# Seven quarter products in six of the 22 half-pairs of an FFN's second matmul

## The chip, the cores and the metric

The kernel runs on one NeuronCore of one Trainium2 chip. The metric is the device time of one execution in microseconds; the time of a kernel is the median of its runs. In code and profile PE is TensorE, PEld its weight loads, DVE VectorE, ACT ScalarE, POOL GpSimd, SP SyncE (which issues the DMAs).

## The reference

One decoder layer on 512 tokens of width 1024, in fp32: a half-step SwiGLU FFN, a token mixer (HGRN2 and mLSTM heads), and a second half-step FFN, each between a pre-norm and a post-norm. What the change touches is the second product of both FFNs, `@ w_out`:

```python
def swiglu_ffn(x, w_in, w_out):          # D_MODEL 1024, D_FF 2816
    gate, up = jnp.split(x @ w_in, 2, axis=-1)
    return (jax.nn.silu(gate) * up) @ w_out

x = x + 0.5 * rms_norm(swiglu_ffn(rms_norm(x, norm_pre[l, 0]), ffn1_w_in[l], ffn1_w_out[l]), norm_post[l, 0])
mixed = token_mixer(rms_norm(x, norm_pre[l, 1]), ...)
x = x + rms_norm(mixed, norm_post[l, 1])
x = x + 0.5 * rms_norm(swiglu_ffn(rms_norm(x, norm_pre[l, 2]), ffn2_w_in[l], ffn2_w_out[l]), norm_post[l, 2])
```

## The kernel before

**Products in two parts.** Each fp32 operand is split into a high part (its cast to fp32r) and a low part (the rest). A product of two such operands is three matmuls: high by high, high by low, low by high (`mm3`, lines 125 to 129). The cast is made by ACT and the residual by DVE: for a weight tile in `split` (L209 the cast, L211 the residual), for a tile of the hidden activations h in `h_tile` (L672 and L673).

**The stages.** `ffn_in` makes gate and up for 11 pairs of 128-row slices of the hidden width (PAIRS = 11), by a scheme of seven products of 256-wide quarters (`prod`, matmuls at L489; `after`, with DVE's additions at L508); GpSimd adds weight quarters for it (L223). The result h lies in `hf`, 22 slices of 128 x 512 tokens. `ffn_out` multiplies it by w_out.

**ffn_out before.** The output's 1024 columns are done in two halves. A half has four PSUM banks (`acc`), one for each tile of 128 tokens. It adds up over the 11 pairs of slices: one pair in one half is a half-pair, so an FFN has 22 of them. A half-pair needs one w tile (two slices by 512 columns, 512 KB) and one h tile, and is 24 matmuls of 128 x 512: four token tiles, two slices, three matmuls each (L127, L128, L129). After the first pair of half 0 the last group of `ffn_in` (`prod("p4", 10)`, 24 matmuls) is done. After half 0, `post0` takes the squares (ACT, L354) and the product with the gain (DVE, L383) from the four banks. The last four pairs of half 1 are done token tile by token tile, with the post-norm and the work of the next stage in between (`last`).

**Buffers.** Loads of w_out go to a ring of five raw tiles (`raw2`), issued by SP. Split weights go to four slots (WBUF = 4): `pull` splits ahead until four are ready or in use, `drop` frees one. Split h tiles go to a ring of three (tag `s`); `more(n)` makes them ahead. `xq` is four tiles that hold the split input of `ffn_in`, free in `ffn_out`. PSUM has eight banks; `ps()` gives the next in turn.

**Order.** Outside the kernel's first part, which is ordered by hand, the order of each engine's instructions is set by a scheduler when the program is built. Each engine then takes its own queue in that order, and waits on semaphores for the other engines.

Of the kernel before, what the change touches and what calls it, by code (L numbers as in the profile page):

```python
# [8 lines left out]
F32 = mybir.dt.float32  # L9
F32R = mybir.dt.float32r  # L10
AF = mybir.ActivationFunctionType
ALU = mybir.AluOpType
PSUM = bass.MemoryType.PSUM

P = 128
T = 512
D = 1024
FF = 2816
NT = T // P
ND = D // P  # L20
NF = FF // P
EPS = 1e-6
RAW, WBUF, PAD, LATE, NEAR = 3, 4, 128, 112, 48
PAIRS = NF // 2
HALF = T // 2
# [4 lines left out]
HQ, HF, HI, HG, MQ, MV, MO, MG = 0, 512, 1024, 1536, 2048, 2560, 3072, 3584  # L30
LEVELS = (1, 64, 32, 16, 8, 4, 2)
TINY = 1e-37
I32 = mybir.dt.int32


# [15 lines left out]
class Load:  # L51


    def __init__(self, key, src, a, b, ring="raw", depth=3, ahead=3, group=None):
        self.key, self.src, self.a, self.b, self.ring, self.depth, self.ahead = key, src, a, b, ring, depth, ahead
        self.group = group


class Item:

    def __init__(self, key, loads, rows=None, adds=(), dst=None):
        self.key, self.loads, self.rows, self.adds, self.dst = key, loads, rows, adds, dst
        self.reads = {key, *(k for pair in adds for k in pair)}


class Layer:
# [26 lines left out]
    def col(self, n=1):  # L95
        return self.sp.tile([P, n], F32, tag=f"col{n}", bufs={1: 12}.get(n, 4), name=self.name("col"))
# [89 lines left out]
    def split(self):  # L186

        nc = self.nc
        it = self.items.popleft()
        raw = self.raw[it.key]  # L190
        _, a, b = raw.shape
        if it.dst:
            w = it.dst()
        else:
            if self.wt is None:
                self.wt = self.wp.tile([P, 2 * D * WBUF + PAD], F32R, name="w")

            taken = {(n, late) for n, late, _ in self.slot.values()}
            fit = [(n, late) for late in (True, False) for n in self.free if (n - 1 if late else n + 1, not late) not in taken]
            n, late = next(f for f in fit if not f[1] or (it.key[0] == "mix" and b == 512))  # L200
            self.free.remove(n)
            o = PAD + 2 * D * n - 16 * late
            w = self.wt[:, o : o + 2 * D].rearrange("p (b k t) -> p b k t", b=2, k=a)
            self.slot[id(w)] = n, late, w
        hi, lo = self.both(w)
        self.ready.append((w, it.dst is not None))
        rows = it.rows
        if rows is None:
            nc.scalar.copy(hi, raw)  # L209
            yield  # L210
            nc.vector.tensor_tensor(lo, raw, hi.bitcast(F32), op=ALU.subtract)  # L211
        else:
            for j in range(a):
                nc.scalar.activation(hi[:, j], raw[:, j], AF.Copy, scale=rows[:, j : j + 1])
            yield
            for j in range(a):
                nc.vector.scalar_tensor_tensor(
                    lo[:, j], raw[:, j], rows[:, j : j + 1], hi[:, j].bitcast(F32), op0=ALU.mult, op1=ALU.subtract
                )
        with self.behind(*self.hold):  # L220
            for out, other in it.adds:
                o, c = self.raw[out], self.raw[other]
                nc.gpsimd.tensor_tensor(o, o, c, op=ALU.add)  # L223
        self.load_due(self.done)
        self.done += 1
        yield
# [44 lines left out]
    def two(self, dst, i, src):  # L271

        v = slice((i % 2) * P, (i % 2 + 1) * P)
        self.nc.scalar.copy(dst[:, 0, :, v], src)
        self.nc.vector.tensor_tensor(dst[:, 1, :, v], src, dst[:, 0, :, v].bitcast(F32), op=ALU.subtract)  # L275
# [398 lines left out]
        return t  # L674

    def ffn_out(self, gpost_row, scale, after, trans, head):
        NK2, LAST = PAIRS, 4
        seq = [k2 for _ in range(2) for k2 in range(NK2)]
        hs = self.hs
        made = [len(hs)]  # L680

        def more(n):
            while made[0] < min(n, len(seq)):
                k2 = seq[made[0]]
                last = made[0] == len(seq) - 1
                dst = self.xq[3].rearrange("p b k t -> p b (k t)").rearrange("p b (k t) -> p b k t", k=2) if last else None
                hs.append(self.h_tile(k2, dst))
                made[0] += 1

        def out_mm(ps, w, h, k2, i):  # L690
            for kk in range(2):
                k = 2 * k2 + kk
                s = slice(i * P, (i + 1) * P)
                self.mm3(ps, h[:, 0, kk, s], h[:, 1, kk, s], w[:, 0, kk, :], w[:, 1, kk, :], k == 0, k == NF - 1)

        g = self.gain("gpost", gpost_row)
        ys = []
        n = 0
        for half in range(2):
            acc = [self.ps() for _ in range(NT)]  # L700
            for k2 in range(NK2 - LAST if half else NK2):
                more(n + 2)
                w = self.pull()
                more(n + 3)
                h = hs.popleft()
                for i in range(NT):
                    out_mm(acc[i], w, h, k2, i)
                self.drop(w)
                n += 1
                if n == 1:  # L710
                    self.prod("p4", PAIRS - 1)
                    self.after("p4", PAIRS - 1)
                self.lag()
            if half == 0:
                ys = [self.post0(acc[i], g, scale) for i in range(NT)]
        ws = []
        for k2 in range(NK2 - LAST, NK2):
            ws.append((k2, self.pull()))
            more(n + 1)
            n += 1  # L720

        def mm(i):
            for m, (k2, w) in enumerate(ws):
                out_mm(acc[i], w, hs[m], k2, i)
                if i == NT - 1:
                    self.drop(w)
                yield LAST - 1 - m

        self.last(mm, ys, acc, g, after, trans, head)


# [73 lines left out]
    def ffn_items(self, name, w_in, w_out):  # L805

        made = []
        place = {"p1": "a", "p2": "c", "p3": "d", "p4": "a", "p5": "a", "p6": "a", "p7": "b"}
        place.update({"c1": "a", "c2": "c", "c3": "b", "c4": "d"})
        adds = {}  # L810
        for t in range(1, PAIRS):
            if t >= HEAD:
                v1, v3 = ("p1", t), ("p4", t - 1)
            elif t > 1:
                v1, v3 = ("p3", t - 1), ("p6", t - 1)
            else:
                v1, v3 = ("p1", 1), ("p1", 2)
            for at, o, i in ((("p5", t), "a", "d"), (("p6", t), "a", "c"), (v1, "a", "b"), (v3, "b", "d")):
                adds.setdefault(at, []).append(((name, t, o), (name, t, i)))

        def load(t, r, group=None):
            ring = ("raw", 3) if t % 2 == 0 and r != "c" else ("raw2", 5)
            k, c = int(r in "cd"), int(r in "bd")
            c0 = c * FF + t * 2 * P
            src = w_in[k * 4 * P : (k + 1) * 4 * P, c0 : c0 + 2 * P].rearrange("(k p) f -> p k f", p=P)
            return Load((name, t, r), src, KH, 2 * P, *ring, 8, group)

        own = {("p1", t): [load(t, r) for r in "abdc"] for t in range(2, PAIRS)}
        own["c1", 0] = [load(t, r, None if (t, r) == (0, "d") else name) for t in range(2) for r in "acbd"]

        stay = {"c1": 1, "c3": 2, "c4": 0}
        for p, t in ORDER:
            if p[0] == "e":
                continue
            dst = (lambda n=stay[p]: self.stay[n]) if p in stay else None
            made.append(Item((name, t, place[p]), own.get((p, t), ()), None, adds.get((p, t), ()), dst))
        for h in range(2):
            for k2 in range(PAIRS):
                src = w_out[k2 * 2 * P : (k2 + 1) * 2 * P, h * 512 : (h + 1) * 512].rearrange("(k p) d -> p k d", p=P)
                key = (name, "out", h, k2)  # L840
                made.append(Item(key, [Load(key, src, 2, 512, "raw2", 5, 8)]))
                if h == k2 == 0:
                    made.append(Item((name, PAIRS - 1, "a"), ()))
        return made

    def small_params(self):

# [31 lines left out]
        self.tiny = mc.tile([P, 1], F32, name="tiny")  # L879
        nc.gpsimd.memset(self.tiny, TINY)  # L880
        self.one = mc.tile([P, 1], F32, name="one")
        nc.gpsimd.memset(self.one, 1.0)

    def masks(self, mc, mb):
# [7 lines left out]
        n16 = len(LEVELS)  # L892
        self.mask = mb.tile([P, n16, 16], I32, name="mask")
        self.eye = mb.tile([P, 32], I32, name="eye")
        wide = self.st("wide", dt=I32)[:, : 64 * n16].rearrange("p (n c) -> p n c", n=n16)
# [663 lines left out]
```

## Time and profile before

| | |
|---|---|
| median of 3 runs | 937.52 us (937.2 to 938.1) |
| the profiled execution | 936.74 us, its span 935.0 us |
| mean granted TensorE clock | 0.998 |
| TensorE busy | 926.7 us (99%) |
| VectorE, ScalarE, GpSimd busy | 700.1, 468.7, 289.9 us |
| w_out loads | 44 of 512 KB, 3.9 us to landing (median) |
| first FFN's ffn_out | 225.3 to about 350 us of the span |

Rows of the timeline are: start, duration, engine, line, operation, output and input with their shapes, and in brackets how long the engine stood idle before it and what ended that. Rows of groups are: line, engine, operation, names, shapes, count, then busy us, mean ns of one, idle us before them and what ended it. Rows of the chain that ended last are: start, length, engine, line, count. Ends of matmuls are modelled, so the distance between starts is the pace. Rows of windows give the stretch, its length, the busy time and count of PE, PEld, DVE, ACT and POOL, the granted clock, the DMA share and GB/s.

### The profile page before, as it was taken

The numbers are of one execution on the slowest core, as the hardware profiler recorded it, in microseconds if no ns is written. First come the engines' busy times: TensorE is split into PE (matmuls) and PEld (weight loads), VectorE is DVE, ScalarE is ACT, GpSimd is POOL, SyncE is SP. The second block draws the span as 40 slices with busy tenths as digits, with TensorE's granted clock in tenths as the row PEclk, the third lists the DMA queues.
The fourth block names the chain that finished last, engine by engine and source line by source line (L and its number), as shares of the span: only waits on it lengthen the run. The fifth ranks groups of instructions, "written<-read, shape, count | busy, mean of one in ns | idle before, by whom it ended". The sixth has DMA issues, their size and how long they took to land.

```text
span 935.0 us, 16820 instructions
## 1 busy us (share of the span) xinstructions
PE 926.7 (99%) x7021; PEld 850.6 (91%) x7021; DVE 700.1 (75%) x785; ACT 468.7 (50%) x639; POOL 289.9 (31%) x225
## 2 busy tenths in 40 slices
PE   9999999999999999999999999999999999999997
PEld 7999999999888889998888888999999999988885
DVE  6798999998545466688766655887999999844543
ACT  7645445455334345987654254853444454534431
POOL 3535555661000027000020301445455655100001
PEclk9999999999999999999999999999999999999999
DMA  9243334425323005422423135213333422332202
GB/s 318 89 136 114 113 97 131 128 99 158 113 91 106 7 3 126 108 83 70 136 70 113 46 108 185 90 46 113 114 111 117 134 91 91 116 110 91 91 0 91
DMA packets 81992, 97.10 MB, mean 104 GB/s; under 512 B 4178, under 2 KB 61558, under 8 KB 81915
## 3 DMA queue, kind: packets, MB, share of 16 engines
q1 hardware_dynamic: 81306, 94.44, 32.4%
q8 instruction: 55, 0.90, 0.4%
q0 software_dynamic: 320, 1.06, 0.3%
q10 hardware_dynamic: 288, 0.52, 0.2%
q14 instruction: 23, 0.18, 0.1%
HBM read 93.90 MB, written 2.11 MB: 103 GB/s over the span
## 4 chain that ended last, share of the span: by engine, by line
PE 97%; DVE 1%; POOL 1%; issue 1%; ACT 1%; DVEq 0%; POOLq 0%; ACTq 0%
PE ps L489 46%; PE ps L127 13%; PE ps L129 13%; PE ps L128 13%; PE ps L434 6%; PE ps L268 1%; PE ps L1058 1%; POOL col L355 0%; PE ps L1328 0%; PE ps L1131 0%; PE ps L1296 0%; PE ps L116 0%; ACT junk L354 0%; PE ps L123 0%; PE ps L1097 0%
## 5 line engine op out<-in xcount | busy, mean ns | idle before, releaser
L211 DVE TENSOR_TENSOR w<-raw,w 128x1024 fp32r<-128x1024 f32 x214 | 364.2, 1710 | 129.5 <-ACT w L209 129.5
L209 ACT CAST w<-raw 128x1024 fp32r<-128x1024 f32 x214 | 223.9, 1052 | 305.6 <-PE ps L129 104.5
L223 POOL TENSOR_TENSOR raw<-raw,raw 128x1024 f32<-128x1024 f32 x80 | 221.0, 2763 | 171.8 <-DVE w L211 161.3
L489 PE MATMUL ps<-xq,w 128*128 128x256 f32 x2016 | 238.1, 277 | 0.0
L489 PEld LDWEIGHTS ps<-xq,w 128*128 128x128 f32 x2016 | 233.7, 188 | 0.2
L489 PE MATMUL ps<-sq,w 128*128 128x256 f32 x1440 | 171.0, 277 | 0.0
L489 PEld LDWEIGHTS ps<-sq,w 128*128 128x128 f32 x1440 | 167.4, 188 | 0.0
L129 PE MATMUL ps<-w,hs 128*128 128x512 f32 x336 | 131.0, 390 | 0.0
L127 PE MATMUL ps<-w,hs 128*128 128x512 f32 x336 | 130.9, 390 | 0.0
L128 PE MATMUL ps<-w,hs 128*128 128x512 f32 x336 | 130.8, 389 | 0.0
L127 PE MATMUL ps<-w,xq 128*128 128x512 f32 x208 | 83.2, 400 | 0.1
L128 PE MATMUL ps<-w,xq 128*128 128x512 f32 x208 | 81.0, 390 | 0.0
L129 PE MATMUL ps<-w,xq 128*128 128x512 f32 x208 | 81.0, 391 | 0.0
L129 PEld LDWEIGHTS ps<-w,hs 128*128 128x128 f32 x336 | 63.1, 188 | 13.8 <-DVE hs L673 0.7
L127 PEld LDWEIGHTS ps<-w,hs 128*128 128x128 f32 x336 | 63.1, 188 | 13.0
L128 PEld LDWEIGHTS ps<-w,hs 128*128 128x128 f32 x336 | 63.1, 188 | 12.8
L355 POOL TENSOR_SCALAR col<-col 128x1 f32<-128x1 f32 x24 | 10.5, 437 | 198.8 <-ACT junk L354 198.6
L434 PE MATMUL ps<-xq,w 128*128 128x256 f32 x480 | 55.8, 278 | 0.0
L434 PEld LDWEIGHTS ps<-xq,w 128*128 128x128 f32 x480 | 55.4, 188 | 0.2 <-issue 0.2
L673 DVE TENSOR_TENSOR hs<-hf,hs 128x1024 fp32r<-128x1024 f32 x42 | 51.1, 1217 | 0.0
L355 POOL TENSOR_SCALAR col<-col,col 128x1 f32<-128x1 f32 x24 | 10.0, 418 | 119.5 <-ACT junk L354 119.2
L129 PEld LDWEIGHTS ps<-w,xq 128*128 128x128 f32 x208 | 39.0, 188 | 8.8 <-DVE xq L275 0.3
(233 smaller groups left out, 939.5 us busy)
## 6 DMA issues: line engine op xcount, KB each, us to landing
raw<-in_ffn_w_in_dram SPq DMA_DIRECT2D x88, 512.0 KB, 4.4
raw<-in_ffn_w_out_dram SPq DMA_DIRECT2D x44, 512.0 KB, 3.9
raw<-in_w_mix_in_dram SPq DMA_DIRECT2D x28, 512.0 KB, 3.8
raw<-in_w_mix_out_dram SPq DMA_DIRECT2D x8, 512.0 KB, 3.7
out_dram<-xs SPq DMA_DIRECT2D x8, 256.0 KB, 2.1
xs<-in_x_dram SPq DMA_DIRECT2D x6, 256.0 KB, 6.2
gpost<-in_norm_post_dram SPq DMA_DIRECT2D x3, 512.0 KB
gpre<-in_norm_pre_dram SPq DMA_DIRECT2D x2, 512.0 KB, 4.1
```

Of the source, the lines that this page charges most:

```text
L127: mm(ps, sh, mh, start=start, stop=False, **kw)
L128: mm(ps, sh, ml, start=False, stop=False, **kw)
L129: mm(ps, sl, mh, start=False, stop=stop, **kw)
L209: nc.scalar.copy(hi, raw)
L211: nc.vector.tensor_tensor(lo, raw, hi.bitcast(F32), op=ALU.subtract)
L223: nc.gpsimd.tensor_tensor(o, o, c, op=ALU.add)
L268: self.nc.tensor.transpose(pt[:, c * P : (c + 1) * P], src[:, k * P : (k + 1) * P], self.ident)
L355: nc.gpsimd.tensor_scalar(m, ss, s2 / D, b, op0=ALU.mult, op1=ALU.add)
L434: mm(ps[:, u0:u1], w[:, a, k, :], self.xop(k, b, u0, u1), start=k + n + m == 0, stop=k == ND - 1 and n == 2, skip_group_check=True,)
L489: self.nc.tensor.matmul(ps[:, c], wb[b][:, k, v], left[d][:, k, :], start=first and a + n + k == 0, stop=n == 2 and k == KH - 1, skip_grou ...
L673: self.nc.vector.tensor_tensor(t[:, 1], src, t[:, 0].bitcast(F32), op=ALU.subtract)
L1058: nc.tensor.matmul(sc[r, o : o + u.stop - u.start], k8[:, m, r], q8[:, m, u], start=True, stop=True, skip_group_check=True)
```

## The change

A table OUT now names for both halves the order and kind of the half-pairs: `p` as before, `k` and `s` by seven quarter products. Half 0 has k3 and k4, half 1 has k3, s1, k4 and s2: six per FFN, twelve in the kernel. Such a half-pair is a 2 x 2 block product (tokens in two halves, the pair's two slices, columns in two halves) made of seven products of blocks, with 42 matmuls 256 wide (`seven`). It needs a second weight tile `wt` of sums of the weight's quarters (`w_sums`: after the first split of a raw tile, four subtractions by DVE in that raw tile, which is then split again into a second slot) and a second h tile of sums (`s_tile`: four DVE steps in `hf`, then a cast and a residual). For k pairs both h tiles are kept in `xq` for both halves.

Products 2, 3 and 4 add straight into the output's banks. Products 1, 5, 6 and 7 add up, over all fast pairs of a half, in four more banks (`sums`). After the last fast pair of a half `gather` makes four terms of them (one ACT copy, four DVE additions, into slices of `hf` that are no longer needed), and at the second p pair after that, p6 in both halves, DVE adds the terms to the output's banks, one addition per bank ahead of that bank's matmuls. `holes()` after half 0 turns the bank ring by four.

No load is added and GpSimd gets no work. The pairs p7 to p10 of half 1 are done as before.

```diff
+OUT = ("p0 p1 p2 k3 k4 p5 p6 p7 p8 p9 p10".split(), "p0 k3 s1 k4 s2 p5 p6 p7 p8 p9 p10".split())
...
 (split)
+        if it.then:
+            it.then(raw)
         self.load_due(self.done)
...
 (ffn_out, more)
+                if kind == "k":
+                    if h == 0:
+                        kept[k2] = self.h_tile(k2, homes.popleft()), self.s_tile(k2, homes.popleft())
+                    hs.append(kept[k2])
+                elif kind == "s":
+                    hs.append((self.h_tile(k2), self.s_tile(k2)))
...
+        def seven(acc, sums, w, wt, h, hs_, stop):
+            tok = lambda q, t: slice(HALF * q + P * t, HALF * q + P * (t + 1))
+            col = lambda q: slice(HALF * q, HALF * (q + 1))
+            for p, a, ka, qa, b, kb, qb in (
+                (1, h, 0, 0, w, 0, 0), (5, hs_, 1, 1, wt, 0, 0), (6, hs_, 0, 0, wt, 1, 1), (7, hs_, 0, 1, wt, 0, 1),
+                (2, h, 1, 0, w, 1, 0), (3, hs_, 1, 0, w, 1, 1), (4, h, 1, 1, wt, 1, 0),
+            ):
+                fresh = p not in sums
+                if fresh and p in (1, 5, 6, 7):
+                    sums[p] = self.ps()
+                for t in range(2):
+                    if p in sums:
+                        out = sums[p][:, col(t)]
+                    else:
+                        out = acc[2 * (p == 4) + t][:, col(p == 3)]
+                    for m, (x, y) in enumerate(((0, 0), (0, 1), (1, 0))):
+                        self.nc.tensor.matmul(
+                            out, a[:, x, ka, tok(qa, t)], b[:, y, kb, col(qb)],
+                            start=p in sums and fresh and t + m == 0, stop=stop and m == 2, skip_group_check=True,
+                        )
+
+        def gather(sums, pairs):
+            x, y = (self.hf[:, 2 * k : 2 * k + 2, :].rearrange("p t (c v) -> p t c v", c=2) for k in pairs)
+            u = self.sp.tile([P, D], F32, tag="xn", bufs=1, name=self.name("u2"))[:, :512]
+            two = lambda t: t.rearrange("p (t v) -> p t v", t=2)
+            self.nc.scalar.copy(x[:, :, 0], two(sums[1]))
+            add(two(u), two(sums[6]), x[:, :, 0])
+            add(x[:, :, 1], two(sums[5]), two(u))
+            add(y[:, :, 0], two(sums[7]), two(u))
+            add(y[:, :, 1], two(sums[5]), y[:, :, 0])
+            return [t[:, i].rearrange("p c v -> p (c v)") for t in (x, y) for i in range(2)]
...
         for half in range(2):
             acc = [self.ps() for _ in range(NT)]
-            for k2 in range(NK2 - LAST if half else NK2):
+            todo = self.outs(half)[: -LAST if half else None]
+            sums, terms, since = {}, None, 0
+            fast = [k2 for _, k2, kind in todo if kind != "p"]
+            for m, k2, kind in todo:
                 more(n + 2)
                 w = self.pull()
+                wt = self.pull() if kind != "p" else None
                 more(n + 3)
-                h = hs.popleft()
-                for i in range(NT):
-                    out_mm(acc[i], w, h, k2, i)
+                h, hs_ = hs.popleft()
+                if kind == "p":
+                    since += terms is not None
+                    for i in range(NT):
+                        if since == 2:
+                            add(acc[i], acc[i], terms[i])
+                        out_mm(acc[i], w, h, i, m == 0, since == 1 or m == PAIRS - 1)
+                else:
+                    seven(acc, sums, w, wt, h, hs_, k2 == fast[-1])
+                    self.drop(wt)
                 self.drop(w)
+                if fast and k2 == fast[-1]:
+                    terms = gather(sums, [k for _, k, kind in self.outs(0) if kind == "k"])
...
             if half == 0:
                 ys = [self.post0(acc[i], g, scale) for i in range(NT)]
+                self.holes()
...
+    def w_sums(self, raw):
+        sub = lambda out, a, b: self.nc.vector.tensor_tensor(out, a, b, op=ALU.subtract)
+        (b11, b12), (b21, b22) = ((raw[:, k, :HALF], raw[:, k, HALF:]) for k in range(2))
+        sub(b11, b12, b11)
+        sub(b12, b22, b12)
+        sub(b22, b22, b11)
+        sub(b21, b21, b22)
+
+    def s_tile(self, k2, dst=None):
+        tt = lambda out, a, b, op: self.nc.vector.tensor_tensor(out, a, b, op=op)
+        (a11, a21), (a12, a22) = ((self.hf[:, 2 * k2 + k, :HALF], self.hf[:, 2 * k2 + k, HALF:]) for k in range(2))
+        tt(a22, a22, a21, ALU.add)
+        tt(a21, a11, a21, ALU.subtract)
+        tt(a11, a22, a11, ALU.subtract)
+        tt(a12, a12, a11, ALU.subtract)
+        return self.h_tile(k2, dst)
```

In the changed file the lines move: a weight's residual is L212, an h tile's L676, `w_sums` L911, `s_tile` L920, the additions of `gather` and into the banks L739, the quarter products' matmuls L723. A weight item with sums stands twice in the list of items, with one load.

More of the change, by code (lines that the diff above doesn't have):

```diff
@@ L59, with __init__ @@
 class Item:
-    def __init__(self, key, loads, rows=None, adds=(), dst=None):
-        self.key, self.loads, self.rows, self.adds, self.dst = key, loads, rows, adds, dst
+    def __init__(self, key, loads, rows=None, adds=(), dst=None, then=None):
+        self.key, self.loads, self.rows, self.adds, self.dst, self.then = key, loads, rows, adds, dst, then
         self.reads = {key, *(k for pair in adds for k in pair)}
@@ L676, in ffn_out @@
     def ffn_out(self, gpost_row, scale, after, trans, head):
-        NK2, LAST = PAIRS, 4
-        seq = [k2 for _ in range(2) for k2 in range(NK2)]
+        LAST = 4
+        seq = [(h, k2, kind) for h in range(2) for _, k2, kind in self.outs(h)]
         hs = self.hs
+        for _ in range(len(hs)):
+            hs.append((hs.popleft(), None))
         made = [len(hs)]
+        flat = lambda q: q.rearrange("p b k t -> p b (k t)").rearrange("p b (k t) -> p b k t", k=2)
+        kept, homes = {}, deque(flat(q) for q in self.xq)
@@ L682, in more @@
         def more(n):
             while made[0] < min(n, len(seq)):
[L684 to L687, printed above, removed]
+                h, k2, kind = seq[made[0]]
+                if kind == "k":
[5 more added lines that the diff above has]
+                else:
+                    hs.append((self.h_tile(k2, flat(self.xq[3]) if made[0] == len(seq) - 1 else None), None))
@@ L688, in more, with out_mm @@
                 made[0] += 1
-        def out_mm(ps, w, h, k2, i):
+        def out_mm(ps, w, h, i, first=False, stop=False):
             for kk in range(2):
-                k = 2 * k2 + kk
                 s = slice(i * P, (i + 1) * P)
-                self.mm3(ps, h[:, 0, kk, s], h[:, 1, kk, s], w[:, 0, kk, :], w[:, 1, kk, :], k == 0, k == NF - 1)
+                self.mm3(ps, h[:, 0, kk, s], h[:, 1, kk, s], w[:, 0, kk, :], w[:, 1, kk, :], first and kk == 0, stop and kk == 1, skip_group_check=True)
@@ L696, in ffn_out @@
+        add = lambda out, a, b: self.nc.vector.tensor_tensor(out, a, b, op=ALU.add)
         g = self.gain("gpost", gpost_row)
@@ L700, in ffn_out @@
             acc = [self.ps() for _ in range(NT)]
-            for k2 in range(NK2 - LAST if half else NK2):
+            todo = self.outs(half)[: -LAST if half else None]
+            sums, terms, since = {}, None, 0
+            fast = [k2 for _, k2, kind in todo if kind != "p"]
+            for m, k2, kind in todo:
                 more(n + 2)
                 w = self.pull()
+                wt = self.pull() if kind != "p" else None
                 more(n + 3)
-                h = hs.popleft()
-                for i in range(NT):
-                    out_mm(acc[i], w, h, k2, i)
+                h, hs_ = hs.popleft()
[5 more added lines that the diff above has]
+                        out_mm(acc[i], w, h, i, m == 0, since == 1 or m == PAIRS - 1)
+                else:
+                    seven(acc, sums, w, wt, h, hs_, k2 == fast[-1])
+                    self.drop(wt)
                 self.drop(w)
+                if fast and k2 == fast[-1]:
+                    terms = gather(sums, [k for _, k, kind in self.outs(0) if kind == "k"])
                 n += 1
@@ L715, in ffn_out @@
                 ys = [self.post0(acc[i], g, scale) for i in range(NT)]
+                self.holes()
         ws = []
-        for k2 in range(NK2 - LAST, NK2):
+        for k2 in range(PAIRS - LAST, PAIRS):
             ws.append((k2, self.pull()))
@@ L723, in mm @@
             for m, (k2, w) in enumerate(ws):
-                out_mm(acc[i], w, hs[m], k2, i)
+                out_mm(acc[i], w, hs[m][0], i, False, m == LAST - 1)
                 if i == NT - 1:
@@ L837, in ffn_items, with outs @@
         for h in range(2):
-            for k2 in range(PAIRS):
+            for n, k2, kind in self.outs(h):
                 src = w_out[k2 * 2 * P : (k2 + 1) * 2 * P, h * 512 : (h + 1) * 512].rearrange("(k p) d -> p k d", p=P)
                 key = (name, "out", h, k2)
-                made.append(Item(key, [Load(key, src, 2, 512, "raw2", 5, 8)]))
-                if h == k2 == 0:
+                made.append(Item(key, [Load(key, src, 2, 512, "raw2", 5, 8)], then=None if kind == "p" else self.w_sums))
+                if kind != "p":
+                    made.append(Item(key, ()))
+                if h == n == 0:
                     made.append(Item((name, PAIRS - 1, "a"), ()))
         return made
+    def outs(self, h):
+        return [(n, int(e[1:]), e[0]) for n, e in enumerate(OUT[h])]
+    def w_sums(self, raw):
[13 more added lines that the diff above has]
+        return self.h_tile(k2, dst)
     def small_params(self):
```

## The prediction

> **What bounds the kernel now.** I read the page's busy shares first, then the slices, then the chain that ended last.
>
> ```profile
> PE 926.7 (99%) x7021; PEld 850.6 (91%) x7021; DVE 700.1 (75%) x785; ACT 468.7 (50%) x639; POOL 289.9 (31%) x225
> DVE  6798999998545466688766655887999999844543
> PE 97%; DVE 1%; POOL 1%; issue 1%; ACT 1%; DVEq 0%; POOLq 0%; ACTq 0%
> ```
>
> TensorE works through 99% of the span and is 97% of the chain, so the time is the sum of its matmuls, and only fewer or cheaper matmuls, or a hole in them, move it. DVE is full in the slices that end each ffn_in and about half full in the slices of ffn_out. How little PE waits is seen in the two lines that the view of PE's waits gives for the whole span, 1.6 us at the start and 0.2 us:
>
> ```profile
> PE ps L123 <- POOL ident masks.py:199: 1.6, 1, 1.6
> PE ps L268 <- DVE hf L373: 0.2, 1, 0.2
> ```
>
> The stage that is changed is ffn_out (from 225.3 us in the first FFN). PE's timeline gives the first matmul of three pairs in a row, and the chain gives the pace of 256-wide matmuls in ffn_in just before:
>
> ```profile
> 233.57 0.39 PE L127 MATMUL ps<-w,hs 128*128 128x512 f32 x1
> ...
> 239.01 0.39 PE L127 MATMUL ps<-w,hs 128*128 128x512 f32 x1
> ...
> 244.45 0.39 PE L127 MATMUL ps<-w,hs 128*128 128x512 f32 x1
> 47.86 177.59 PE ps L489 x1560
> ```
>
> A pair of 24 matmuls takes 5.44 us, 226.7 ns each; a 256-wide matmul is paced at 177.59/1560 = 113.8 ns, just half.
>
> **The feed of a pair in ffn_out.** ACT casts the next w once a slot is free, DVE makes its residual, and the same for h:
>
> ```profile
> 210.19 3.04 DVE L211 TENSOR_TENSOR w<-raw,w 128x1024 fp32r<-128x1024 f32 x1
> 239.25 1.05 ACT L209 CAST w<-raw 128x1024 fp32r<-128x1024 f32 x1 [1.45 <-PE ps L129]
> 232.03 1.23 DVE L211 TENSOR_TENSOR w<-raw,w 128x1024 fp32r<-128x1024 f32 x1 [2.57 <-ACT w L209]
> 240.34 1.23 DVE L211 TENSOR_TENSOR w<-raw,w 128x1024 fp32r<-128x1024 f32 x1 [1.28 <-ACT w L209]
> 241.48 1.22 DVE L673 TENSOR_TENSOR hs<-hf,hs 128x1024 fp32r<-128x1024 f32 x1
> 245.78 1.22 DVE L211 TENSOR_TENSOR w<-raw,w 128x1024 fp32r<-128x1024 f32 x1 [3.08 <-ACT w L209]
> L211 DVE TENSOR_TENSOR w<-raw,w 128x1024 fp32r<-128x1024 f32 x20 | 24.5, 1223 | 49.6 <-ACT w L209 49.6
> L673 DVE TENSOR_TENSOR hs<-hf,hs 128x1024 fp32r<-128x1024 f32 x19 | 23.1, 1218 | 0.0
> L209 ACT CAST w<-raw 128x1024 fp32r<-128x1024 f32 x20 | 21.0, 1052 | 57.8 <-PE ps L129 46.8 <-issue 10.3 <-PE ps L489 0.7
> L383 DVE TENSOR_TENSOR y<-ps,gpost 128x512 f32<-128x512 f32 x4 | 2.7, 687 | 0.9 <-ACT junk L354 0.9
> ```
>
> The last four rows group ffn_out alone (225.5 to 343 us). From these rows: the cast starts 0.24 us after the pace of the pair before ends (239.01, 239.25), takes 1.05; the residual starts 0.04 after the cast (240.30, 240.34) and takes 1.22; the next DVE step that waits for nothing starts 0.09 before that one ends (240.34 + 1.23 to 241.48). So DVE does 1.14 + 1.14 per pair of 5.44, and idles 3.08.
>
> **The change part by part.** *Matmuls.* A fast half-pair has 7 x 3 x 2 = 42 matmuls of 256 columns for 24 of 512: 42 x 113.8 = 4.78 us for 5.44, a gain of 0.66. Twelve of them are in the two FFNs: 7.9 us, 3.96 per FFN, of it 1.32 in half 0 (k3, k4) and 2.64 in half 1 (k3, s1, k4, s2). All lies on the path.
>
> *Transfers* are unchanged: the same 44 loads of w_out, and GpSimd gets nothing.
>
> *DVE and ACT per fast pair.* A second w slot (wt) needs four subtractions of 128x256 in the raw tile, then a second cast and residual; the s tile needs four such steps, a cast and a residual. The trace has no such 128x256 step of two SBUF operands. It has these on either side, and two of DVE's dependent steps:
>
> ```profile
> L1309 DVE SCALAR_TENSOR_TENSOR y<-ps,col,y 128x128 f32<-128x128 f32 x16 | 4.7, 344 | 4.9 <-POOL col L260 4.9
> L1350 DVE TENSOR_TENSOR y<-ps,col 128x256 f32<-128x256 f32 x8 | 3.0, 420 | 6.6 <-POOL col L1347 6.6
> 508.82 0.15 DVE L1341 SCALAR_TENSOR_TENSOR col<-col 128x4 f32<-128x4 f32 x1
> 509.00 0.16 DVE L1342 TENSOR_TENSOR col<-col,emT 128x4 f32<-128x4 f32 x1
> ```
>
> I take 0.42 us, by the row of the same size, with bounds 0.30 and 0.50; a dependent step starts 0.03 to 0.04 after the one before it ends. So wt's residual comes, after the first cast of the same raw tile starts, 1.05 + 0.04 + 1.22 + 4 x 0.46 + 1.05 + 0.04 + 1.22 = 6.5 us later: longer than the 4.78 us that a fast pair lasts. One fast pair after another cannot be fed at full pace with four slots of which each takes two.
>
> I laid the steps of the order in which the changed program is built, engine by engine, each with its row's duration and no earlier than what it waits for.
>
> *Half 0.* At the end of ffn_in DVE is full, and the sums and residuals of k3 and k4 come on top: 16 steps of 0.37 net and four residuals of 1.14, 10.5 us, against idle stretches of 2.57 + 1.28 + 3.08 us in the rows above and some 1 us between. k3 (from 244.45) is fed about 0.9 us ahead. k4's wt residual ends at 250.6, and PE asks for it 7 matmuls into k4, at 244.45 + 4.78 + 0.80 = 250.03: 0.6 us lost, between 0 (short steps) and 1.7 (if residuals there stretch like the one of 3.04 us at 210.19, in ffn_in). The bank additions at p6 come without loss: k3 and k4 are followed by p5, whose w and h stand ready.
>
> *Half 1,* from S, the start of its p0: k3 from S+5.44 and s1 from 10.22 are fed in time. k4 takes the slots that k3 leaves at 10.22: cast to 11.51, residual to 12.77, subtractions to 14.6, cast to 15.7, residual to 16.96, while k4 starts at 15.0 and wants it 12 matmuls on, at 16.37: 0.6 lost. k4 then ends at 20.4. The built order interleaves p5's matmuls with s2's. p5's h residual stands behind a tile that waits for k4's end (23.7, 0.85 lost), s2's wt residual comes at 27.45 (0.9 lost). p5 ends at T = S+32.4.
>
> *The bank additions of half 1.* p6's first matmul now waits for DVE's addition into its bank. In DVE's queue that addition stands behind residuals for later pairs:
>
> ```
> gather (4 additions), between them the h residual for p6
> w residual, h residual for p7
> w residual for p8: its cast waits for the slot of p5's last matmul
> h residual for p8: its tile waits for p5's last matmul
> addition into bank 0  <- p6's first matmul waits
> ```
>
> So a residual that nobody needs for 10 us holds the addition, and it cannot start before p5 ends. From waits alone: 0.24 + 1.05 + 0.04 + 1.14 + 1.14 + 0.69 (L383's kind, bank operand) + 0.05 = 4.36 us of empty PE. The gather and the residuals ahead end only at T+2.5, as s2's late end delays them, and with them the addition ends at T+5.4. I take 5.4; the walk gives 5.4 for any step between 0.30 and 0.50. The other three additions run 0.6 us apart, ahead of PE's 1.36 per bank. Behind the waiting addition stands the p9 residual, which loses nothing that PE feels while it stands still: 0.1 for the tail.
>
> Sum per FFN: -3.96 + 0.6 + 0.6 + 0.85 + 0.9 + 5.4 + 0.1 = +4.5; twice, +9.0 us. The second FFN has the same built order. The profiled execution took 936.74 (span 935.0), 0.78 below the median of 937.52: 945.7 on its basis, **946.5** on the median's. With steps of 0.30 and no loss in half 0 the walk gives +3.1 per FFN (943.8); with 0.50 and 1.7 lost, +6.3 (950.1).
>
> A PE that has stood still is another matter. The trace has no pause of PE after 1.6 us that is longer than 0.2, so nothing in it shows a restart but the start of the span itself. [...]
>
> **Rivals.** *Slow restart.* The start of the span shows PE slow for some time:
>
> ```profile
> 1.56 1.22 PE ps L123 x4
> 8.07 1.94 PE ps L268 x8
> 10.01 0.58 PE ps L123 x4
> 20.47 0.87 PE ps L268 x8
> 0.00:5.00 5.00, 3.44 (x7) 2.09 (x8) 0.18 (x1) 1.84 (x3) 0.85 (x8) 1.00 0.59 189
> ```
>
> The same L268 transposes take 242 ns each at 8.07 and 109 ns at 20.47. From 1.56 to about 10.0 PE ran at some 0.45 of its later pace, at most 8.4 x 0.55 = 4.6 us lost. If each of the two holes brings such a start back, between 0 and 4.6 us each, half of it taken: 946.5 + 2 x 2.3 = 951.1. Against it: the granted clock of that window reads 1.00, so what slowed PE there may be the empty queues and DMA of a start. [...]
>
> *Slower matmuls.* The first 72 matmuls of ffn_in ran slower than the later 1560:
>
> ```profile
> 11.71 8.77 PE ps L489 x72
> ```
>
> At 121.8 ns a fast pair takes 5.12 and gains 0.33: 4 us less, 950.5. Against it: 1560 in a row at 113.8, of the same shape. For it: the banks alternate differently here.
>
> *Not slower.* DVE has nothing left ahead of p8's residual when p5 ends, and the four waits of 0.6 to 0.9 us are covered, so only the 4.36 stays: 2 x (4.36 + 0.1 - 3.96) = +1.0, 938.5. It decides where the 128x256 step is well under 0.30 us and the gather is done before p5 ends. For it: DVE is idle 3.08 of 5.44 us in this stage before. Against it: even at 0.30 the walk leaves 1.6 us of the waits and the whole of the 5.4.
>
> *The addition doesn't wait* as I read it (the chip's queue gets past the two residuals before p5 ends, or PE has other work there): without the 5.4, 937.52 + 2 x (4.5 - 5.4) = 935.7, faster. I see nothing for it.
>
> **How the numbers follow.** A difference of 0.2% (1.9 us) is about what can be told from none. Forecast 0.47, slow restart 0.32, slower matmuls 0.08, not slower 0.08, no wait 0.05. The first three are slower, the fourth the same, the last faster. The forecast's own range is 943.8 to 950.1; up to 953.0 it takes in most of the slow restart and the slower matmuls, and 942.5 gives the lower end a little room towards the fourth. Left out are the last two cases and the top of the second, some 0.2.
>
> **What would show it.** In the trace after: the L723 matmuls, 42 per fast pair, paced at 113.8 (slower matmuls: 118 to 122). PE's waits, now 0.2 after the start, must show one of about 5.4 us per FFN at p6 of half 1, put down to the L739 addition, and in DVE's timeline the addition must follow a w and an h residual that start 1.3 us or more after PE stopped. Small waits of 0.5 to 1 us at k4, p5 and s2, on DVE's residuals. After the hole, matmuls at 226.7 ns say that the restart is not slow; some 450 ns for 3 us or more say that it is. The prediction is wrong if PE runs through p6, or if the losses between the fast pairs are several us instead of 0.6 to 0.9.

## The result: 951.0 us, 1.5% slower

The changed kernel takes 951.03 us (median of 4 runs, 950.9 to 953.5) against 937.36 us before (936.9 to 938.1), a ratio of 1.0151 (95% interval 1.0134 to 1.0169), 13.7 us more. The profiled execution is the longest of the four, 953.48 us with a span of 951.6, and its first ffn_out starts 1.1 us later than before (p0 at 226.42 instead of 225.29), ahead of anything that the change touches. Two executions among the experiments below were disturbed, one of spread (1019.4 us at a clock of 0.85) and one of mt (1909.5 us), and the ratios leave them out.

Page of the changed kernel, busy shares, slices and the chain by engine:

```profile
PE 929.7 (98%) x7237; PEld 860.3 (90%) x7237; DVE 766.4 (81%) x913; ACT 485.7 (51%) x659; POOL 289.4 (30%) x225
DVE  6798999999858756788766655887999999986853
PEclk9999999999999899999999999999999999999989
PE 88%; DVE 7%; issue 2%; ACT 1%; DMA 0%; POOL 0%; DVEq 0%; POOLq 0%; SPq 0%; ACTq 0%
```

PE was 97% of the chain and is 88%; DVE was 1% and is 7%. PE's busy time did not fall, it rose from 926.7 to 929.7 us. The granted clock has an 8 in one slice near the end of each FFN. PE's waits tell where:

```profile
engine line waited for: us in total, times, longest us
PE ps L128 <- DVE ps L739: 10.5, 2, 5.3
PE ps L124 <- POOL ident masks.py:199: 1.6, 1, 1.6
PE ps L723 <- DVE w L212: 1.5, 4, 0.6
PE ps L129 <- DVE w L212: 0.8, 2, 0.4
...
```

Two waits of 5.25 us for the bank addition (L739), one in each FFN; four of 0.2 and 0.6 us for the residual of the second weight tile, at k4 and s2 of half 1; and two of 0.4 us at p5 for the residual of its own weight tile. The timeline of PE in the first FFN: p0 of half 0, then half 1's k3, s1 and k4, the end of p5 and the start of p6, and the mixer's first long row:

```profile
226.42 0.39 PE L128 MATMUL ps<-w,hs 128*128 128x512 f32 x1
...
293.99 5.11 PE L723 MATMUL ps<-w,xq 128*128 128x256 f32 x42
298.94 5.19 PE L723 MATMUL ps<-w,hs 128*128 128x256 f32 x42
303.97 1.52 PE L723 MATMUL ps<-w,xq 128*128 128x256 f32 x12
305.68 3.81 PE L723 MATMUL ps<-w,xq 128*128 128x256 f32 x30 [0.18 <-DVE w L212]
...
321.16 0.39 PE L130 MATMUL ps<-w,hs 128*128 128x512 f32 x1
326.80 0.77 PE L128 MATMUL ps<-w,hs 128*128 128x512 f32 x1 [5.25 <-DVE ps L739]
327.37 0.63 PE L129 MATMUL ps<-w,hs 128*128 128x512 f32 x1
327.80 0.63 PE L130 MATMUL ps<-w,hs 128*128 128x512 f32 x1
...
332.90 0.39 PE L130 MATMUL ps<-w,hs 128*128 128x512 f32 x1
333.13 0.40 PE L128 MATMUL ps<-w,hs 128*128 128x512 f32 x1
...
372.68 34.84 PE L437 MATMUL ps<-xq,w 128*128 128x256 f32 x306
```

Three things stand here. k3 takes 4.95 us (293.99 to 298.94, 117.9 ns per matmul) and s1 5.03 (119.8 ns). The hole lasts from 321.39, where p5's last matmul has had its 0.23, to 326.80: 5.41 us. And after it matmuls start 427 ns apart instead of 227, for 14 of them, until 332.90: 6.10 us for what takes 3.17, 2.9 us lost. In the second FFN the hole has the same length, from 909.84 to 915.25, and the slow matmuls are 11:

```profile
910.00:915.00 5.00, 0.00 (x0) 0.00 (x0) 5.00 (x5) 1.99 (x2) 0.00 (x0) 0.81 0.00 0
326.05:332.87 6.82, 6.07 (x14) 4.79 (x15) 2.40 (x4) 0.00 (x0) 0.00 (x0) 0.50 0.00 0
913.15:919.97 6.82, 4.72 (x11) 3.79 (x12) 3.75 (x6) 0.00 (x0) 0.00 (x0) 0.50 0.00 0
```

These are windows: the granted clock (the third number from the end) falls within the hole and is still 0.50 (the half clock below) while PE works again, for 6.82 us in both FFNs; it falls 4.7 us behind p5's end in the first and 3.3 us in the second, and so 14 and 11 matmuls lie in it. DVE is busy through all of the hole (5.00 of 5.00). Its timeline there, first FFN:

```profile
320.82 0.69 DVE L739 TENSOR_TENSOR hf<-ps,hf 128x512 f32<-128x512 f32 x1
321.42 1.22 DVE L212 TENSOR_TENSOR w<-raw,w 128x1024 fp32r<-128x1024 f32 x1
322.56 1.22 DVE L676 TENSOR_TENSOR hs<-hf,hs 128x1024 fp32r<-128x1024 f32 x1
323.69 1.22 DVE L212 TENSOR_TENSOR w<-raw,w 128x1024 fp32r<-128x1024 f32 x1
324.83 1.22 DVE L676 TENSOR_TENSOR hs<-hf,hs 128x1024 fp32r<-128x1024 f32 x1
325.96 2.49 DVE L739 TENSOR_TENSOR ps<-ps,hf 128x512 f32<-128x512 f32 x4
```

The last step of the gather starts at 320.82; then come w and h of p7, w and h of p8, and only then the four additions. The PE rows are enough to add up the first FFN, from p0's first matmul to the first of the mixer's 306 matmuls. After, that stretch goes from 226.42 to 372.68 (above). PE's timeline of the kernel before has the same two places at:

```profile
225.29 0.39 PE L127 MATMUL ps<-w,hs 128*128 128x512 f32 x1
...
363.53 34.84 PE L434 MATMUL ps<-xq,w 128*128 128x256 f32 x306
```

138.24 us has become 146.26, +8.0: six fast half-pairs gain 4 x 0.49 + 2 x 0.41 = 2.8, and against that stand 0.4 at k4 of half 0, 0.5 + 0.7 + 0.8 at k4, p5 and s2 of half 1 (starts against the pace, so somewhat above the waits as listed), 5.4 for the hole and 2.9 for the slow matmuls after it.

The waits at k4 and at p5 of half 1 have different reasons. These are some of the steps of ACT and DVE ahead of the two:

```profile
299.14 1.05 ACT L210 CAST w<-raw 128x1024 fp32r<-128x1024 f32 x1 [2.94 <-PE ps L723]
301.48 1.80 DVE L911 TENSOR_TENSOR raw<-raw 128x256 f32<-128x256 f32 x4
303.32 1.05 ACT L210 CAST w<-raw 128x1024 fp32r<-128x1024 f32 x1 [3.13 <-DVE raw L911]
304.40 1.23 DVE L212 TENSOR_TENSOR w<-raw,w 128x1024 fp32r<-128x1024 f32 x1 [1.11 <-ACT w L210]
...
308.69 1.05 ACT L675 CAST xq<-hf 128x1024 fp32r<-128x1024 f32 x1 [1.48 <-PE ps L723]
309.77 1.23 DVE L676 TENSOR_TENSOR xq<-hf,xq 128x1024 fp32r<-128x1024 f32 x1
311.25 1.22 DVE L212 TENSOR_TENSOR w<-raw,w 128x1024 fp32r<-128x1024 f32 x1
```

At k4 it is the length of the second weight tile's chain: from the first cast at 299.14 to the end of the second residual at 305.63 it takes 6.5 us, and DVE stood idle for 1.11 us just ahead of that residual; k4 goes on at 305.68. Behind that, DVE has no gap from 304.40 to 316.22. p5's residual (311.25) stands there behind a residual into `xq` (309.77) that is first read at 339.93, by the last pair's matmuls, and whose cast waited for k4's matmuls.

### The profile page after: what moved, and what is told of

Its sections match the earlier page's. It is cut to its first block, busy times and chain, and to the rows that moved or that the text cites. A ratio compares the mean times of both kernels' runs of the same rounds, so it can differ in the third digit from the quotient of the medians.

```text
span 951.6 us, 17416 instructions
## 1 busy us (share of the span) xinstructions
PE 929.7 (98%) x7237; PEld 860.3 (90%) x7237; DVE 766.4 (81%) x913; ACT 485.7 (51%) x659; POOL 289.4 (30%) x225
## 4 chain that ended last, share of the span: by engine, by line
PE 88%; DVE 7%; issue 2%; ACT 1%; DMA 0%; POOL 0%; DVEq 0%; POOLq 0%; SPq 0%; ACTq 0%
PE ps L492 43%; PE ps L128 10%; PE ps L130 10%; PE ps L129 10%; PE ps L437 6%; PE ps L723 4%; DVE w L212 3%; PE ps L271 1%; PE ps L447 1%; DVE hs L676 1%; DVE raw L911 1%; PE ps L1140 1%; ACT w L210 1%; DVE xq L676 1%; PE ps L1410 0%
## 5 line engine op out<-in xcount | busy, mean ns | idle before, releaser
L212 DVE TENSOR_TENSOR w<-raw,w 128x1024 fp32r<-128x1024 f32 x226 | 373.5, 1663 | 76.0 <-ACT w L210 75.9
L210 ACT CAST w<-raw 128x1024 fp32r<-128x1024 f32 x226 | 235.5, 1052 | 279.6 <-POOL raw L224 89.6
L128 PE MATMUL ps<-w,hs 128*128 128x512 f32 x240 | 95.8, 400 | 10.5 <-DVE ps L739 10.5
L129 PE MATMUL ps<-w,hs 128*128 128x512 f32 x240 | 95.8, 399 | 0.8 <-DVE w L212 0.8
L130 PE MATMUL ps<-w,hs 128*128 128x512 f32 x240 | 95.4, 397 | 0.0
L128 PEld LDWEIGHTS ps<-w,hs 128*128 128x128 f32 x240 | 46.1, 193 | 20.5 <-issue 11.3
L129 PEld LDWEIGHTS ps<-w,hs 128*128 128x128 f32 x240 | 46.4, 193 | 11.0 <-DVE w L212 1.7
L130 PEld LDWEIGHTS ps<-w,hs 128*128 128x128 f32 x240 | 46.3, 193 | 10.5 <-DVE hs L676 0.7
L676 DVE TENSOR_TENSOR hs<-hf,hs 128x1024 fp32r<-128x1024 f32 x38 | 46.3, 1220 | 1.2 <-ACT hs L675 1.2
L675 ACT CAST hs<-hf 128x1024 fp32r<-128x1024 f32 x38 | 39.9, 1049 | 14.1 <-PE ps L723 8.7
```

Source lines behind the costliest of these rows:

```text
L128: mm(ps, sh, mh, start=start, stop=False, **kw)
L129: mm(ps, sh, ml, start=False, stop=False, **kw)
L130: mm(ps, sl, mh, start=False, stop=stop, **kw)
L675: self.nc.scalar.copy(t[:, 0], src)
L676: self.nc.vector.tensor_tensor(t[:, 1], src, t[:, 0].bitcast(F32), op=ALU.subtract)
```

## The experiments

All medians are against the kernel before on the same chip, 937.4 us.

**early** and **late** move the bank additions in the program, and with them in DVE's queue.

```diff
 early: behind p5's matmuls             late: behind p6's matmuls
-                        if since == 2:
-                            add(acc[i], acc[i], terms[i])
                         out_mm(acc[i], w, h, i, m == 0, ...)
+                        if since == 1:                  # late: since == 2
+                            add(acc[i], acc[i], terms[i])
```

> Edit: the bank additions are issued bank by bank right behind p5's matmuls instead of ahead of p6's. As built they then stand ahead of p8's w and h residuals, and behind p7's. Queue theory (the 5.4 us hole at p6 comes from the residuals that stand ahead of the addition): p7's h residual ended 2.4 us after p5's last matmul, so the hole is 2.4 + 0.6 + 0.05 = 3.1 us, 2.3 less per FFN: 951.0 - 4.6 = 946.4 us, or, if a hole of 3.1 us no longer brings the half clock, another 1.8 us less per FFN, 942.8. Backlog theory (VectorE has simply more work there than time, whatever the order): the hole stays near 5.4 and the time near 951.

948.09 us (943.9 to 948.6), ratio 1.0103 (1.0082 to 1.0125). PE's timeline:

```profile
321.14 0.39 PE L130 MATMUL ps<-w,hs 128*128 128x512 f32 x1
324.51 0.76 PE L128 MATMUL ps<-w,hs 128*128 128x512 f32 x1 [2.98 <-DVE ps L739]
325.07 0.63 PE L129 MATMUL ps<-w,hs 128*128 128x512 f32 x1
```

The hole is 3.1 us, as the queue theory had it to a tenth, so the residuals ahead of the addition do set it. Only the two residuals of p8 are off the front; with p7's two still ahead, more than half of the hole stays. The time is 1.7 us above 946.4, a sum that has the half clock in it at 1.8 us per FFN, an estimate (spin, below, has 1.7). In the profiled execution the half clock came after this hole of 3.1 us too (the granted clock from 320 to 340 us is 0.83, as in the changed kernel), for 14 matmuls in the first FFN and 8 in the second, 2.9 and 1.7 us lost, which is 1.0 of the 1.7. Three executions lie at 947.8 to 948.6 with mean clocks of 0.993 and 0.994; the one at 943.92, 4.5 us below the profiled one (948.41), shows 0.999, as the kernels without slow matmuls do.

> Edit: the bank additions are issued behind p6's matmuls, bank by bank, so that the first to wait for them is p7 of bank 0. p8's residuals then run while PE works on p6 (5.44 us). Queue theory: no hole at p6, at most 0.5 us at p7, no half clock: 951.0 - 2 x 5.4 - 2 x 1.8 = 936.6, up to 937.6 us. Backlog theory: the hole moves to p7 or p8 and is still 3 us or more: 943 us or more.

937.23 us, ratio 0.9998 (0.9989 to 1.0007). DVE's timeline:

```profile
324.36 1.22 DVE L676 TENSOR_TENSOR hs<-hf,hs 128x1024 fp32r<-128x1024 f32 x1
325.50 2.49 DVE L739 TENSOR_TENSOR ps<-ps,hf 128x512 f32<-128x512 f32 x4
```

DVE does the same steps in the same order as in the changed kernel, at the same distance behind the gather. Only the matmuls that wait for the additions come one half-pair later. No wait on L739 is left among PE's, and all 13.8 us are gone. VectorE's amount of work is not what made the hole; which matmul waits for the end of its queue is.

**spin** keeps PE at work in the hole.

```diff
                         if since == 2:
+                            for _ in range(20 if half and i == 0 else 0):
+                                self.nc.tensor.matmul(sums[1], h[:, 0, 0, :P], h[:, 0, 0, :], start=True, stop=True, ...)
                             add(acc[i], acc[i], terms[i])
```

> Edit: 20 matmuls of 128x512 into a bank that is no longer read are put on PE ahead of p6 in half 1 of both FFNs; they do no useful work and fill 4.5 of the 5.4 us in which PE waits. The addition that p6 waits for is as in the changed kernel. If it is PE's standing still that brings the half clock: p6 starts as late as before but at 227 ns per matmul, 1.8 us less per FFN: 951.0 - 3.6 = 947.4 us. If something else slows the matmuls there (VectorE's additions in PSUM beside them, say): 951 us.

947.71 us (947.5 to 947.9), ratio 1.0108 (1.0091 to 1.0125):

```profile
320.83 4.70 PE L759 MATMUL ps<-hs 128*128 128x512 f32 x20
326.15 0.50 PE L128 MATMUL ps<-w,hs 128*128 128x512 f32 x1 [0.63 <-DVE ps L739]
326.49 0.39 PE L129 MATMUL ps<-w,hs 128*128 128x512 f32 x1
326.72 0.40 PE L130 MATMUL ps<-w,hs 128*128 128x512 f32 x1
```

p6 starts 5.32 us after p5's end, as without the edit, beside the same additions, and runs at 227 ns: the granted clock from 320 to 340 us is 1.00, where the changed kernel has 0.83. So PE's pause brings the half clock, and it costs 951.03 - 947.71 = 3.3 us in the median, 1.7 per FFN. That may be up to 0.7 too little: k4 of half 0 in the first FFN lost 1.1 us in this profiled execution (a wait of 0.83 us) and 0.4 in the changed kernel's.

**half0** has fast half-pairs in half 0 alone. Its half 1 reads slices 3 and 4 of h after half 0 has put sums there, so its output isn't the reference's.

```diff
-OUT = (..., "p0 k3 s1 k4 s2 p5 p6 p7 p8 p9 p10".split())
+OUT = (..., "p0 p1 p2 p3 p4 p5 p6 p7 p8 p9 p10".split())
```

> Edit: fast half-pairs in half 0 alone (k3, k4), half 1 as before the change. The changed kernel's trace gives half 0 a gain of 0.57 us per FFN (10.29 us for k3 and k4 instead of 10.88). Theory: 937.4 - 2 x 0.57 = 936.2 us, since half 1 holds the whole loss; 940 us or more if the loss also comes from half 0 (DVE full at the end of ffn_in).

937.44 us, ratio 1.0000 (0.9991 to 1.0009). The loss is in half 1, as expected, but the gain of half 0 is not there:

```profile
PE ps L128 <- DVE ps L739: 0.4, 2, 0.2
```

In this kernel p6 of half 0 waits for its additions (0.4 us in the two FFNs in this view, 0.5 per FFN by starts against the pace in the first), and that takes most of the 0.57. What is left is less than the interval (0.8 us to either side) can tell.

**nosubs** and **mt** stand on `late` and ask for the size of the gain.

```diff
-made.append(Item(..., then=None if kind == "p" else self.w_sums))
+made.append(Item(..., then=None if kind == "p" else (lambda raw: None)))
```

> Edit on the kernel 'late': the four subtractions of w_sums are left out, so that wt is the split of the weight itself and the output isn't the reference's; casts, residuals, slots and matmuls stay. Theory: the small waits between fast half-pairs (in 'late' 0.4 us at k4 of half 0, and 0.5, 0.7 and 0.9 us in half 1, 2.4 us per FFN) are the length of wt's chain, cast, residual, four subtractions, cast, residual. 1.8 us shorter, all of them go: 937.2 - 4.8 = 932.4 us. Rival: the slots set them (two of four for each fast half-pair), then they stay for the most part: 936 to 937 us.

931.70 us, ratio 0.9941 (0.9926 to 0.9956). All that is left in PE's waits:

```profile
PE ps L124 <- POOL ident masks.py:199: 1.6, 1, 1.6
PE ps L271 <- DVE hf L376: 0.2, 1, 0.2
```

Every wait in the fast half-pairs is gone with the 1.8 us of subtractions, though slots, casts and residuals are as they were. So the slots do not set the waits. wt's chain is 6.5 us long with the subtractions and 4.7 without them, against the 4.95 of a half-pair, which is the reason at k4. At p5 and s2, where DVE had no gap, this run does not tell the chain's length from the time that the subtractions take in DVE's queue. The kernel is 5.5 us faster than `late`, most of it the waits (2.3 to 2.4 us per FFN by starts), and they are what left `late` no faster than the kernel before.

```diff
-                for t in range(2):
-                    ...
-                    for m, (x, y) in enumerate(((0, 0), (0, 1), (1, 0))):
+                for m, (x, y) in enumerate(((0, 0), (0, 1), (1, 0))):
+                    for t in range(2):
```

> Edit on the kernel 'late': in the quarter products the loop over the two token tiles lies inside the loop over the three partial products, so that consecutive matmuls go to different halves of a bank. The changed kernel's trace has the 256-wide matmuls of these half-pairs at 118 to 120 ns where 113.8 was forecast. If three matmuls in a row into the same 256 columns cause that, the pace falls to 114: 42 x 0.005 = 0.2 us for each of 12 half-pairs, 937.2 - 2.4 = 934.8 us. If it lies in the operands (where h is held), 937.2 us.

937.21 us, ratio 1.0000 (0.9990 to 1.0010). The matmuls stay at 118 and 120 ns: the order of bank halves is not the reason. Nor is the place of h alone. The 118 are mostly found with h in `xq` and the 120 with h in the ring `s`, but here are k4 and s2 of half 1 in nosubs:

```profile
302.92 4.92 PE L723 MATMUL ps<-w,xq 128*128 128x256 f32 x42
307.68 5.20 PE L723 MATMUL ps<-w,hs 128*128 128x256 f32 x42
```

k4 takes 4.76 us, 113.3 ns per matmul, from the same tiles of `xq` with which k3 and k4 of half 0 take 117.7 on average. In the changed kernel's second FFN the first 12 matmuls of k4 in half 1 start 113 to 114 ns apart and the 30 behind its wait about 118, with h in the same tiles. What sets the pace stays open. mt's profiled execution (938.62 us) shows something else:

```profile
313.26 1.32 PE L723 MATMUL ps<-w,hs 128*128 128x256 f32 x8 [1.64 <-ACT w L210]
314.38 0.63 PE L129 MATMUL ps<-w,hs 128*128 128x512 f32 x1
314.81 0.63 PE L130 MATMUL ps<-w,hs 128*128 128x512 f32 x1
...
317.37 0.89 PE L723 MATMUL ps<-w,hs 128*128 128x256 f32 x5
```

The new built order has a wait of 1.64 us here, and even behind that comes a stretch of 427 ns matmuls, 3.0 us long, beginning about 1 us after PE was back; the granted clock from 310 to 320 us is 0.83. The same execution has a second such wait (3.3 us for the two in PE's waits, the longest 1.64), in the second FFN, and that brought none.

**spread**, **spread2** and **best** put ordinary half-pairs between those of quarter products, on `late`.

```diff
 spread:  half 0  p0 p1 p2 k3 k4 p5 p6 p7 p8 p9 p10    half 1  p0 k3 p1 k4 p2 p5 p6 p7 p8 p9 p10
 spread2: half 0  p0 p1 k3 p2 k4 p5 p6 p7 p8 p9 p10    half 1  as spread
 best:    half 0  p0 p1 p2 k3 p5 k4 p6 p7 p8 p9 p10    half 1  as spread
```

> Edit on the kernel 'late': half 1 is p0 k3 p1 k4 p2 p5 p6, so s1 and s2 are ordinary and no two fast half-pairs follow each other in half 1; half 0 as in the change. Theory (one fast half-pair after another can't be fed with four slots): the waits of half 1 go, 0.4 us stays at k4 of half 0. Four fast half-pairs at 4.95 instead of 5.44: per FFN -1.96 + 0.4 = -1.6, 937.4 - 3.2 = 934.2 us, fewer fast half-pairs and yet faster than 'late'. Rival (the waits come from VectorE's total work): 936 us or more.

934.47 us, ratio 0.9969 (0.9958 to 0.9981). Four fast half-pairs per FFN are faster than the six of late, by 2.8 us.

> The kernel 'spread' a second time, since the profiled execution of its first run was disturbed and can't be read: 934.5 us, waits of 0.4 us at k4 of half 0 and none in half 1.

934.17 us, ratio 0.9966 (0.9954 to 0.9978). After the start of the span PE's waits list nothing at all. By starts against the pace, 0.37 us is lost at k4 of half 0 and nothing between the fast half-pairs of half 1.

> Edit on 'spread': half 0 is p0 p1 k3 p2 k4 p5 and on, so that an ordinary half-pair lies between k3 and k4 there too. Theory: the last wait of 0.4 us goes, 937.4 - 2 x 1.96 = 933.5 us. Rival: k3 now comes one pair nearer to the end of ffn_in, where VectorE is full, and waits there: 934 to 936 us.

935.08 us, ratio 0.9976 (0.9967 to 0.9985): the rival. k3 now waits for DVE's end of ffn_in:

```profile
PE ps L723 <- DVE hf L511: 1.1, 2, 0.9
```

> Edit on 'spread': half 0 is p0 p1 p2 k3 p5 k4 p6 and on: k3 keeps its place, and an ordinary half-pair lies between k3 and k4. Theory: in 'spread' only the wait at k4 of half 0 is left, 0.4 us per FFN, and in 'spread2' k3 came too early instead (1.0 and 0.4 us lost). Without both: 934.5 - 0.8 = 933.7 us. Rival: the remaining loss isn't there, and it stays at 934.5.

933.35 us (933.2 to 933.8), ratio 0.9958 (0.9945 to 0.9972), 0.35 us better than expected. This version is faster than both kernels, by 4.1 us than the one before. It has the same half-pairs as spread and so the same work for VectorE, in another order, and its executions all lie below those of spread on the same chip (934.0 to 934.6): in half 0 the spacing is what counts.

## Why the prediction was right

The time lies in the range, and the change went the way and the distance of the prediction's second case rather than its first: 951.0, where the slow restart gave 951.1 and the forecast 946.5.

- *The hole at p6.* Forecast T+5.4, measured 5.41 in both FFNs, with the steps of DVE in the order that the built program gave: shown by the rows, by early (3.1 us when two of the four residuals come off the front) and by late (none).
- *The small waits.* Forecast 0.6, 0.6, 0.85 and 0.9 us per FFN, measured 0.4 (0.3 in the second FFN), 0.5, 0.7 and 0.8. That the four subtractions make them is shown by nosubs. At k4 the reason is that wt's chain is longer than a half-pair, by the rows and by best; spread takes the waits of half 1 away with the spacing and with some of VectorE's work at once. The wait at p5 is for the residual of its w and not, as forecast, of its h, though behind a tile that waits for k4's matmuls, as forecast. And it is not the four slots that keep fast half-pairs from following each other, as the prediction has it: nosubs has four. The 128x256 step was 423 ns against 420 assumed.
- *The gain of a fast half-pair* is the mis-sized term: 0.49 and 0.41 us instead of 0.66, since its matmuls start 117.9 and 119.8 ns apart and not 113.8. Per FFN 2.8 instead of 3.96, 2.4 us in the two. The rival of slower matmuls had the direction, and somewhat too much of it (121.8 against 118 to 120), and its chance of 0.08 was too low for something that the first 72 matmuls of ffn_in had shown. The x1560 were not a safe row to carry over: k4 in nosubs runs at their pace and the others do not, and no run shows why.
- *The restart* is the step that parted forecast and result. It costs 3.3 us by spin, 1.7 per hole in the median; I had it at 4.6 (a rival with 0.32), an estimate from the start of the span alone. The profiled execution lost 2.9 and 2.3. That the clock row read 1.00 at the span's start was no argument against it: the first record of the clock in the trace before stands at 10.17 us, where PE's slow start ends, and in front of it the view shows 1.00 for want of a record.
- 947.71 without the half clock is 1.2 above the forecast of 946.5: about 2.4 for the gain, less 1.2 for the small waits (2.95 per FFN forecast, 2.4 and 2.3 measured).

So the direction came from the right wait, the distance from two terms that were both too low, the gain's loss and the restart. That the slow restart's 951.1 meets the 951.0 is luck: its 4.6 us are 1.3 too many, and the gain's loss less the small waits, which it does not have, is 1.2.

## What to carry to other kernels

A step that a saturated engine waits for has to be looked up in the built order of the engine that makes it: an addition of 0.7 us cost 5.4 because four residuals for the two pairs after p6 stood ahead of it (without p8's two it cost 3.1), and moving the matmul that waits was enough. When PE is the bound, a pause can cost more than its length (5.4 us here, and 2.9 and 2.3 more in the profiled execution's two FFNs), so a change that trades matmuls for work on other engines should be laid out so that no feed chain (here 6.5 us against 4.95) runs back to back: four well-spaced fast half-pairs gave 4.1 us where six back to back gave nothing (late).

## What was not expected of the hardware

Waits much shorter than the hole brought the half clock as well. After 5.25 us of waiting there were 14 matmuls at 427 ns in one FFN and 11 in the other, after 2.98 us 14 and 8, and after 1.64 us (with PE busy for 9.81 of the 10 us from 300) 7 of 512 columns at that pace in one FFN, starting a microsecond after PE was back, and none in the other. The waits under 1 us did not bring it: up to 0.9 us in spread2, 0.8 in spin and 0.6 in late, whose profiled executions have a mean clock of 0.999.

In the changed kernel the clock stood at 0.50 from 326.05 to 332.87 and from 913.15 to 919.97, 6.82 us both times. It fell 4.7 and 3.3 us behind p5's end, in two holes of the same length, and came back 6.07 and 4.72 us after PE's first matmul. In early the mean of 0.83 from 320 to 340 us comes to 6.8 us at 0.50, and in mt that of 0.83 from 310 to 320 us to 3.4. So the length of a wait does not settle alone whether the clock falls, when, and for how many matmuls. Executions of one kernel differ in it too: three of mt's have a mean clock of 0.997 and take 938.5 to 938.6 us, six have 0.998 or 0.999 and take 936.6 to 937.2. What else settles it was not shown; no run moved a pause to test it.

Matmuls of 256 columns have paces of 113, 118 and 120 ns, with the same tiles of h at 113 and at 118, and not by the order of their outputs; the reason is open.
